# Attention with the keys on the partitions: row maxima by a product of high parts, no transposed probabilities, sums on GpSimd, one scaling per output

## The chip, the cores and the metric

The kernel runs on one core of a Trainium2 chip. A time is the device time of that core in microseconds (us), from the first to the last instruction of one launch with a small rest around it. A kernel's time is the median of several launches. Below, PE is TensorE (matmuls, with a separate engine row PEld for its weight loads), DVE is VectorE, ACT is ScalarE, POOL is GpSimd, and SP is the engine that issues most DMA transfers.

## What is computed

The reference is one layer of a hybrid network: 1024 latent tokens and 256 prompt tokens, width 1024, float32. A normalised and modulated input goes through one wide projection, then through two token mixers side by side (a gated linear recurrence called HGRN here, and attention), an output projection, and a squared-ReLU MLP. The change is in the attention:

```python
s = jnp.einsum('bqkgd,bskd->bkgqs', qi, kf) * scale   # 8 query heads on 2 key/value heads, 64 wide
p = jax.nn.softmax(s, axis=-1)
return jnp.einsum('bkgqs,bskd->bqkgd', p, vf)
```

Latent queries attend to 512 cached keys and the 1024 latent keys (1536 in all); prompt queries attend to the 256 prompt keys.

The kernel's matmuls take their operands in a format that the code calls F32R. A float32 operand x is split into a high part hi(x), which is x copied to that format, and a low part x - hi(x). A product of two split operands is three matmuls: high by high, high by low, low by high. With heads of 64 channels the kernel puts both parts of an operand on top of each other on 128 partitions, and gets the product with two matmuls.

## The kernel before

The program is built by one function. The order of PE's instructions is the order of the code; the instructions of the other engines and of the DMA queues are ordered by a scheduler that follows estimated times. Each engine runs its own list strictly in order, and waits at the first instruction whose operands or buffers are not ready.

The stages, in order: a front part (normalisation, the projection of keys, values and half of the queries), the projection of the other queries, the attention, the HGRN recurrence, output projections, the MLP, and the final normalisation. The matmuls of the attention and of HGRN are mixed with others: a "filler" is a generator that gives out the remaining parts of the wide projection (`z_ch`, `z_tok`, lines 316 to 347) a few matmuls at a time. `attention(fill)` (lines 787 to 811) makes a list of events, each with a due time in steps, sorts it, and before each event lets the filler advance to the same share of its total. So a stretch of PE's list holds attention matmuls and, evenly between them, filler matmuls (L312 to L314 and L329 to L331).

A `Unit` (lines 664 to 766) is one head and 256 queries, with the queries on the partitions. There are 32 units for latent queries and 8 for prompt queries. In a latent unit:

- `score`: for each block of 128 queries and each of three groups of 512 keys, two matmuls write 128 x 512 scores (L697), and DVE takes the maximum of each row (L698, L702).
- `expo`: ACT takes the exponential with the negative maximum as bias, and adds up the row (L708); DVE makes the reciprocal of the sum (L711, L712).
- `norm`: the exponentials are multiplied by that reciprocal, alternately on POOL and DVE (L716).
- `trans`: for two key blocks of 128 and two query blocks, four PE transposes (L738) bring the keys onto the partitions in PSUM; ACT copies the high part out (L741), DVE makes the low part (L742).
- `value`: high and low parts are multiplied with the values, 256 queries wide (L753, L754), and added up in one PSUM bank. At a unit's end ACT and DVE add the two halves of the result (L762, L763).

PSUM has eight banks, in three rings: "g" with three (filler, and the sum in `value`), "s" with three (scores), "t" with two (transposes). SBUF tiles come from rings too, with a buffer used again when its last reader is done. Ring X holds 20 tiles of 128 x 512 (keys and exponentials among them). Ring K holds a single tile: first `ident0`, then `R`, a constant pattern that the scans of HGRN read (L1091 to L1093, L874, L875). HGRN's preparation (`prep`, lines 865 to 931) runs on DVE and POOL and ends in the tile `usf`, which PE transposes in `keys_t` (L936) before any other matmul of that stage. The filler of HGRN (L1094) comes after that in PE's list.

## Time and profile before

| | |
|---|---|
| median of 3 runs (lowest to highest) | 2095.98 us (2095.45 to 2096.78) |
| the profiled execution's own time | 2093.83 us |
| its span, first to last instruction | 2092.1 us |
| mean granted PE clock | 0.995 |
| PE / DVE / ACT / POOL busy | 97% / 67% / 46% / 26% |
| first and last score matmul (L697) starts | 186.1 us, 730.2 us |
| last value matmul (L754) starts | 745.6 us |
| first HGRN scores (L947) start | 754.5 us |

The profile is one execution on the chip. The table of windows gives, for stretches of that execution, each engine's busy time. A group is all instructions of one line, engine and shape: count, then total busy us and mean ns of one, then the idle time of the engine just before them and who ended it. The chain is the work that ended last, followed back from the end, so its entries show what a matmul costs when the next one follows at once: PE is a pipeline, and the 390 ns of a matmul of 512 columns overlap with the next one's.

### The profile page before, as it was taken

To read this page: it belongs to the slowest core of one execution; us is meant where nothing else is said; L and a number is where in the kernel's file an instruction comes from. 1 tells how busy PE (TensorE), PEld (TensorE's weight loads), DVE (VectorE), ACT (ScalarE), POOL (GpSimd) and SP (SyncE) were. 2 spreads that over 40 slices of the span, in tenths; PEclk is the share of its full clock that TensorE was granted. 3 is DMA by queue.
4 is the path that set the end of the run, shared out by engine and by line. 5 is a ranking of instruction groups with operands and counts; after the bars stand their busy time and mean duration, and the time that the engine had idled before them with its cause. 6 is when DMAs were issued, how large, how long until landed. Compare 5 with 4: busy or idle time off the path is not lost.

```text
span 2092.1 us, 33337 instructions
## 1 busy us (share of the span) xinstructions
PE 2035.8 (97%) x12244; PEld 1748.0 (84%) x12244; DVE 1405.6 (67%) x2653; ACT 952.0 (46%) x1961; POOL 540.3 (26%) x577
## 2 busy tenths in 40 slices
PE   6899999999999999999999999999999999999998
PEld 4788889988889978888888888988888888888876
DVE  4784676776776797778354735776666666577686
ACT  4754555555565522322231425654454544333442
POOL 1472232333323355455212200222211210000010
PEclk9999999999999999999999999999999999999999
DMA  9455220232221355445644523774444479545773
GB/s 295 130 165 168 74 76 31 77 116 69 78 74 37 107 164 175 139 146 158 216 145 140 206 101 99 218 215 149 157 146 156 157 254 365 166 154 177 228 252 124
DMA packets 230243, 319.19 MB, mean 153 GB/s; under 512 B 18072, under 2 KB 148720, under 8 KB 230080
## 3 DMA queue, kind: packets, MB, share of 16 engines
q1 hardware_dynamic: 217664, 277.41, 41.4%
q0 software_dynamic: 12416, 39.66, 5.3%
q8 instruction: 96, 1.57, 0.3%
q14 instruction: 67, 0.55, 0.1%
HBM read 229.43 MB, written 87.57 MB: 152 GB/s over the span
## 4 chain that ended last, share of the span: by engine, by line
PE 83%; DVE 8%; DMA 5%; ACT 2%; issue 1%; SPq 0%; POOL 0%; DVEq 0%; POOLq 0%; ACTq 0%
PE ps_g L312 7%; PE ps_g L314 7%; PE ps_g L313 7%; PE ps_s L697 4%; PE ps_t L738 4%; PE ps_g L1591 2%; PE ps_g L1589 2%; PE ps_g L1590 2%; PE ps_g L754 2%; PE ps_s L1437 2%; PE ps_s L1438 2%; PE ps_s L1439 2%; DMA wraw<-in_w_ff 2%; PE ps_g L329 2%; PE ps_g L753 2%; PE ps_g L331 2%
## 5 line engine op out<-in xcount | busy, mean ns | idle before, releaser
L312 PE MATMUL ps_g<-hs,wsp 128*128 128x512 f32 (+1 forms) x896 | 322.3, 360 | 0.1
L314 PE MATMUL ps_g<-hs,wsp 128*128 128x512 f32 (+1 forms) x896 | 309.5, 345 | 0.8 <-DVE wsp L284 0.8
L313 PE MATMUL ps_g<-hs,wsp 128*128 128x512 f32 (+1 forms) x896 | 309.0, 345 | 0.0
L716 POOL TENSOR_SCALAR pexp<-pexp,rs 128x512 f32<-128x512 f32 (+1 forms) x104 | 170.2, 1643 | 375.6 <-ACT pTh L741 190.8
L283 ACT ACTIVATE wsp<-wraw 128x1024 fp32r<-128x1024 f32 x110 | 109.6, 998 | 262.8 <-PE ps_g L313 81.0
L284 DVE TENSOR_TENSOR wsp<-wraw,wsp 128x1024 fp32r<-128x1024 f32 x110 | 134.3, 1223 | 120.8 <-ACT wsp L283 120.4
L314 PEld LDWEIGHTS ps_g<-hs,wsp 128*128 128x128 f32 x896 | 169.3, 189 | 22.7 <-DVE wsp L284 1.0
L312 PEld LDWEIGHTS ps_g<-hs,wsp 128*128 128x128 f32 x896 | 169.7, 189 | 21.2 <-issue 4.6
L313 PEld LDWEIGHTS ps_g<-hs,wsp 128*128 128x128 f32 x896 | 170.0, 190 | 15.3
L741 ACT ACTIVATE pTh<-ps_t 128x512 fp32r<-128x512 f32 x200 | 118.9, 601 | 122.3 <-PE ps_t L738 119.3
L698 DVE TENSOR_REDUCE mx<-ps_s 128x1 f32<-128x512 f32 (+1 forms) x208 | 137.0, 663 | 53.9 <-PE ps_s L697 53.4
L283 ACT ACTIVATE ah<-ar 128x640 fp32r<-128x640 f32 (+1 forms) x112 | 80.9, 723 | 187.4 <-PE ps_g L1590 102.3
L708 ACT ACTIVATE pexp<-ps_s,ngm 128x512 f32<-128x512 f32 (+1 forms) x208 | 137.4, 669 | 43.2 <-DVE ngm L702 41.7
L742 DVE TENSOR_TENSOR pTl<-ps_t,pTh 128x512 fp32r<-128x512 f32 x200 | 136.0, 681 | 15.8 <-ACT pTh L741 15.4
L284 DVE TENSOR_TENSOR ah<-ar,ah 128x640 fp32r<-128x640 f32 (+1 forms) x112 | 90.1, 805 | 77.2 <-ACT ah L283 76.0
L697 PE MATMUL ps_s<-Kl,Ql 128*128 128x512 f32 (+1 forms) x416 | 128.9, 415 | 1.6 <-ACT pexp L708 1.6
L738 PE MATMUL ps_t<-ident,pexp 128*128 128x128 f32 x800 | 120.7, 273 | 2.5 <-DVE ngm L702 1.3
L329 PE MATMUL ps_g<-wsp,hs 128*128 128x256 f32 x400 | 117.5, 294 | 0.0
L331 PE MATMUL ps_g<-wsp,hs 128*128 128x256 f32 x400 | 113.7, 284 | 0.0
L330 PE MATMUL ps_g<-wsp,hs 128*128 128x256 f32 x400 | 113.6, 284 | 0.0
L754 PE MATMUL ps_g<-pTl,Vl 128*128 128x256 f32 x400 | 106.2, 286 | 3.6 <-DVE pTl L742 3.5
L753 PE MATMUL ps_g<-pTh,Vl 128*128 128x256 f32 x400 | 106.1, 285 | 1.3 <-DVE oa L763 1.1
(417 smaller groups left out, 5443.5 us busy)
## 6 DMA issues: line engine op xcount, KB each, us to landing
ar<-AF SPq DMA_DIRECT2D x112, 320.0 KB, 3.5
wraw<-in_w_ff SPq DMA_DIRECT2D x32, 1024.0 KB, 6.4
wr<-in_w_ff SPq DMA_DIRECT2D x128, 256.0 KB, 4.5
wraw<-in_w_in SPq DMA_DIRECT2D x18, 1024.0 KB, 5.5
wraw<-in_w_ada SPq DMA_DIRECT2D x16, 1024.0 KB, 5.5
AF<-a POOLq DMA_DIRECT2D x48, 256.0 KB, 2.8
AF<-t POOLq DMA_DIRECT2D x48, 256.0 KB, 2.3
wa<-in_w_ada SPq DMA_DIRECT2D x32, 256.0 KB, 5.8
```

Source lines behind the costliest of these rows:

```text
L283: s_.activation(hi, raw, AF.Copy)
L284: v.tensor_tensor(lo, raw, f32(hi), op=ALU.subtract)
L312: pe.matmul(out, hi[:, k, :], mh, start=(first and k == 0), stop=False)
L313: pe.matmul(out, hi[:, k, :], ml, start=False, stop=False)
L314: pe.matmul(out, lo[:, k, :], mh, start=False, stop=(last and k == kcs - 1))
L329: pe.matmul(po[:, bb, :], mh[:, off:off + P], wh[:, k % 4, :], start=(k == 0), stop=False)
L331: pe.matmul(po[:, bb, :], ml[:, off:off + P], wh[:, k % 4, :], start=False, stop=(k == KC - 1))
L697: pe.matmul(pq[:, 0:n], self.qh[:, q0:q0 + P], K[self.g][var][self.kts[i]], start=(var == 0), stop=(var == 1))
L716: NORM[(i + j) % len(NORM)].tensor_scalar(x, x, self.rs[j], None, op0=ALU.mult)
L738: pe.transpose(pt[:, a, j * P:(j + 1) * P], self.Ps[j][i][:, b * P:(b + 1) * P], ident)
L753: pe.matmul(pv[:, 0:256], V[self.g][kg][:, b, :], hi[:, a, :], start=(k == 0), stop=False)
L754: pe.matmul(pv[:, 0:256], V[self.g][kg][:, b, :], lo[:, a, :], start=False, stop=(k == last))
```

## The change

A unit now has the keys on the partitions, so no probability is transposed. There are 16 latent units of one head and 512 queries, with 12 key blocks of 128 each, and 4 prompt units of two heads and 256 queries each, with 2 key blocks: 200 blocks in all. In a unit:

- `top`: one matmul per 128 queries and key group, high parts of the keys by both parts of the queries (L707), and a DVE maximum of each row (L708). That is close to the true maximum, and only has to keep the exponential in range.
- `top_row`: a PE transpose turns the four columns of negative maxima into rows (L715), ACT copies them (L717), and four small DMAs write them into partition 64 of a second query operand `q2` (L719). `q2` holds the high part of the queries on partitions 0 to 63 and zeros below row 64; the low-part operand of the keys holds the low part, a row of ones and zeros. So the second score matmul adds low by high and the negative maximum.
- `score`: per key block two matmuls of 512 queries (L725), the exponential without bias or sum (L727), the high part by ACT from SBUF (L729), the low part by DVE from SBUF (L730). POOL adds the exponentials up over the blocks (L735, L737).
- `value`: high and low part by the values, 512 wide (L748), in a PSUM bank of its own ("v"); ring "g" has two banks during the attention.
- `sums`: four matmuls with one column (L759) add POOL's tile over the partitions; DVE takes the reciprocal. `scale`: a PE transpose (L766), an ACT copy into the tile `prow`, a DMA to memory and a DMA that spreads it to 64 partitions, both issued by POOL (L109, L772), and one POOL product with the unit's output (L773).

In the front part the high and low parts of the keys are made differently, three of the eight scalings of the prompt columns go from DVE to ACT, and the priority of one split is lowered. The norm weights `qkw`, `mrow` and `prow` share ring K with `ident0` and `R`.

```diff
-    PSB = {"g": 3, "s": 3, "t": 2}
+    PSB = {"g": 2, "v": 1, "s": 3, "t": 2}
...
-            if kc % 3 == 1:
+            if kc % 3 == 1 and t < 2:
...
-        v.tensor_tensor(st[:, :, 1], kb, f32(st[:, :, 0]), op=ALU.subtract)
+        v.tensor_tensor(st[:, :, 1, 0], kr, f32(st[:, :, 0, 0]), op=ALU.subtract)
+        s_.activation(st[:, :, 1, 1], one0.unsqueeze(1).broadcast_to([P, 2, 64]), AF.Copy)
...
-            with tc.high_priority(offset=600):
+            with tc.high_priority(offset=0):
...
+        def top(self, b, i):
...
+            pq = PS("t")
+            pe.matmul(pq[:, 0:n], self.q1[:, b * P:(b + 1) * P], K[self.g][0][self.kts[i]], start=True, stop=True)
+            v.tensor_reduce(self.mx[:, i:i + 1], pq[:, 0:n], axis=AX.X, op=ALU.max)
...
+        def top_row(self):
+            pt = PS("t")
+            pe.transpose(pt[0:4, 0:P], self.ngm, ident)
+            r = S((4, P), F32R, name="mrow")
+            s_.activation(r, pt[0:4, 0:P], AF.Copy)
+            for b in range(4):
+                dma(self.q2[64:65, b * P:(b + 1) * P], r[b:b + 1, :])
...
+        def score(self, k):
+            kg, b = self.kt[k]
+            pq = PS("s")
+            for var, q in enumerate((self.q1, self.q2)):
+                pe.matmul(pq, K[self.g][var][kg][:, b * P:(b + 1) * P], q, start=(var == 0), stop=(var == 1))
+            e = S(name="pexp")
+            s_.activation(e, pq, AF.Exp)
+            hi, lo = S(dt=F32R, name="pTh"), S(dt=F32R, name="pTl%d" % (k % 2))
+            s_.activation(hi, e, AF.Copy)
+            v.tensor_tensor(lo, e, f32(hi), op=ALU.subtract)
...
+                g_.tensor_tensor(self.acc, self.acc, e, op=ALU.add)
...
+        def scale(self):
+            pt = PS("t")
+            pe.transpose(pt[0:4, 0:P], self.rs, ident)
+            r = S((4, P), name="prow")
+            s_.activation(r, pt[0:4, 0:P], AF.Copy)
+            row = RR[self.h][self.t]
+            store(row.rearrange("o (b n) -> (o b) n", b=4), r)
+            o, rb = self.o, S((64, 512), name="prb")
+            g_.dma_start(out=rb, in_=row.broadcast_to([64, 512]))
+            g_.tensor_tensor(o, o, rb, op=ALU.mult)
...
+            ev += [(-12.9, u.load_q, ()), (-5.9, u.load_q2, ()), (-2.9, u.top_row, ())]
+            tops = [(b, i) for b in range(4) for i in range(len(u.kts))]
+            ev += [(-11.6 + 8.2 * j / len(tops), u.top, x) for j, x in enumerate(tops)]
+            ev += [(k, u.score, (k,)) for k in range(u.nb)]
+            ev += [(2 * p2 + 3.6, u.value, (p2,)) for p2 in range(u.nb // 2)]
+            ev += [(u.nb + 3.3, u.sums, ()), (u.nb + 4.3, u.scale, ())]
```

The numbers ahead of the events are due times in steps of one key block, counted from the unit's first score.

PE in the middle of the attention, before: value matmuls (L753, L754), four transposes of exponentials (L738), two scores of two matmuls each (L697), and filler (L312 to L314).

```order
L753 MATMUL ps_g<-pTh,Vl 128x256 [waits Activation_49]
L754 MATMUL ps_g<-pTl,Vl 128x256 [waits DVE_49]
L753 MATMUL ps_g<-pTh,Vl 128x256
L754 MATMUL ps_g<-pTl,Vl 128x256
L738 MATMUL ps_t<-ident,pexp 128x128 [waits PE_49]
L738 MATMUL ps_t<-ident,pexp 128x128 x3
L697 MATMUL ps_s<-Kl,Ql 128x512 [waits DMAHW7_49,DMAHW4_49,Activation_49]
L697 MATMUL ps_s<-Kl,Ql 128x512 [waits DMAHW0_49]
```

The same engine in the changed kernel: scores (L725) of one key block, values 512 wide (L748), the first block of the next unit with its second operand (Q_5293), and a matmul for a maximum (L707).

```order
L725 MATMUL ps_s<-Ql,Kl 128x512
L725 MATMUL ps_s<-Q_4953,Kl 128x512
L318 MATMUL ps_g<-hs,wsp 128x512
L319 MATMUL ps_g<-hs,wsp 128x512
L320 MATMUL ps_g<-hs,wsp 128x512
L748 MATMUL ps_v<-pTh,Vl 128x512 [waits Activation_49]
L748 MATMUL ps_v<-pTl_5336,Vl 128x512 [waits DVE_49]
L748 MATMUL ps_v<-pTh,Vl 128x512 [waits Activation_49]
L748 MATMUL ps_v<-pTl_5359,Vl 128x512 [waits DVE_49]
L725 MATMUL ps_s<-Ql,Kl 128x512
L725 MATMUL ps_s<-Q_5293,Kl 128x512 [waits DMAHW3_49,DMAHW4_49,DMAHW2_49,DMAHW7_49,DMAHW1_49,DMAHW0_49]
```

The transposes and the narrow value matmuls are gone, and a unit's first score waits for DMAs (the row of maxima among them).

POOL's list before, early in the program: the two memsets of `R` stand between the loads of the masks and the normalisation of the first rows (L254).

```order
L145 DMA mask_115<-const_masks 128x128
L891 MEMSET um 128x4x16 x2
L1092 MEMSET R 128x512
L254 TENSOR_TENSOR rst<-mm,mexp 128x4
L1093 MEMSET R 128x16
```

POOL's list of the changed kernel at the end of the attention: the last sums (L737), the last two DMAs of `scale` (RR_1_1951 is the row in memory, prb its copy on 64 partitions), the memsets of `R` (L1109, L1110), and the first products of HGRN (L900, L928) around the last scaling (L773).

```order
L737 TENSOR_TENSOR pacc<-pacc,pexp 128x512 [waits Activation_49,Pool_49] x3
L868 TENSOR_TENSOR ze<-ze,hnb 128x512 [waits DMAHW6_49,DVE_49]
L109 DMA RR_1_1951<-prow 4x128 [waits Activation_49]
L868 TENSOR_TENSOR ze<-ze,hnb 128x512 [waits DMAHW7_49,DVE_49]
L772 DMA prb<-RR_1_1951 64x512 [waits DMASW0_49,PE_49]
L1109 MEMSET R 128x512 [waits DMAHW4_49,DMAHW3_49,DMAHW5_49,DMAHW2_49,DMAHW6_49,DMAHW1_49,DMAHW0_49]
L1110 MEMSET R 128x16 [waits Pool_49]
L900 TENSOR_SCALAR uf<-uf 128x512 [waits DMAHW6_49,DVE_49,PE_49]
L773 TENSOR_TENSOR oa<-oa,prb 64x512 [waits DMAHW2_49,DMASW1_49]
L928 TENSOR_TENSOR usf<-uf,usf 128x512 [waits DVE_49,Pool_49]
```

`R` has moved from the start of POOL's list to behind the last `prow` of the attention, because both are in ring K.

SP's list of the changed kernel around the row of maxima of one unit (Q_4953 is its `q2`, QS the stored queries, OA the stored outputs of earlier units, KS the stored keys).

```order
L106 DMA Q_4953<-QS_1_139 64x512 [waits DMAHW5_49,PE_49,Activation_49]
L106 DMA OA_2_1928<-oa 64x2x256 [waits DMAHW6_49,Pool_49]
L106 DMA Q_4953<-mrow 1x16x8 [waits DMAHW7_49,Activation_49]
L106 DMA Q_4953<-mrow 1x16x8 [waits DMAHW0_49]
L106 DMA Q_4953<-mrow 1x16x8 [waits DMAHW1_49]
L106 DMA Q_4953<-mrow 1x16x8 [waits DMAHW2_49]
L106 DMA Kl<-KS_141 128x512 [waits DMAHW3_49,DMASW1_49,DVE_49]
```

The four small DMAs are new, and ahead of them stands a store that waits for POOL's product of an earlier unit.

More of the change, by code (lines that the diff above doesn't have):

```diff
@@ L618, in build @@
                 front_prep(evs)
[L619 removed]
+            banks = [PS(x) for x in ("sssv", "ggss", "sv")[t]]
         cols_next = t == 0 and kc % 2 == 1 and kc < KC - 1
@@ L765, in value @@
-            if self.h % 2 == 1 and self.q2 == n // 256 - 1:
-                dma(OA[self.h // 2][self.t], o_at[self.h // 2, self.t][:, 0:n])
-    NORM = [g_, v]
-    q_at, o_at = {}, {}
+                self.pv = PS("v")
+            last = self.nb - 1
+            for k in (2 * p2, 2 * p2 + 1):
+                kg, b = self.kt[k]
+                for j, x in enumerate(self.pt.pop(k)):
+                    pe.matmul(self.pv, V[self.g][kg][:, b, :], x, start=(k == 0 and j == 0), stop=(k == last and j == 1))
@@ new lines, in value, with sums @@
+            if k == last:
+                tm, self.o = S((64, 512), name="pvt"), S((64, 512), name="oa")
+                with tc.high_priority(offset=400):
+                    s_.activation(tm, self.pv[64:128], AF.Copy)
+                    v.tensor_tensor(self.o, self.pv[0:64], tm, op=ALU.add)
+        def sums(self):
+            pt = PS("t")
+            for b in range(4):
+                pe.matmul(pt[:, b:b + 1], self.acc[:, b * P:(b + 1) * P], one0[:, 0:1], start=True, stop=True)
+            self.rs = T(4, "rs")
+            v.reciprocal(self.rs, pt[:, 0:4])
```

180 lines of the change are left out of this document (66 added, 114 removed), and 5 rows, old and new, of the table RING_OF.

## The prediction

> **What bounds the kernel now.** I read the page first, then the table of windows around the attention, then the chain inside it.
>
> ```profile
> PE 2035.8 (97%) x12244; PEld 1748.0 (84%) x12244; DVE 1405.6 (67%) x2653; ACT 952.0 (46%) x1961; POOL 540.3 (26%) x577
> 196.00:740.00 544.00, 536.82 (x3788) 485.30 (x3788) 383.83 (x834) 308.48 (x734) 180.52 (x113) 1.00 0.22 73
> 740.00:755.00 15.00, 11.09 (x81) 8.95 (x85) 14.84 (x27) 4.68 (x10) 9.88 (x9) 0.89 0.54 180
> 755.00:1025.00 270.00, 267.63 (x2169) 226.16 (x2162) 211.61 (x492) 74.35 (x191) 136.85 (x160) 1.00 0.51 161
> ```
>
> The window rows hold length, then busy time of PE, PEld, DVE, ACT and POOL, the clock, DMA. In the attention (196 to 740 us) PE is busy 536.8 of 544 us, DVE 71%, POOL 33%; in HGRN (755 to 1025) PE is busy 267.6 of 270. So a matmul less in the attention shortens the program, and a wait of PE at its end lengthens it one to one. Busy time hides short gaps, so I cost matmuls by the chain, where an entry is the time until the next matmul starts:
>
> ```profile
> 602.32 0.44 PE ps_t L738 x4
> 602.76 0.94 PE ps_s L697 x4
> 603.70 0.23 PE ps_g L312
> ...
> 731.98 0.11 PE ps_g L753
> 732.09 0.12 PE ps_g L754
> ```
>
> 512 columns cost 0.23 us, 256 columns 0.12, and a bundle of four transposes 0.44.
>
> **The change on PE.** The groups give the counts:
>
> ```profile
> L697 PE MATMUL ps_s<-Kl,Ql 128*128 128x512 f32 x384 | 121.9, 424 | 1.6 <-ACT pexp L708 1.6
> L697 PE MATMUL ps_s<-Kl,Ql 128*128 128x256 f32 x32 | 7.1, 302 | 0.0
> L738 PE MATMUL ps_t<-ident,pexp 128*128 128x128 f32 x800 | 120.7, 273 | 2.5 <-DVE ngm L702 1.3 <-DVE pexp L716 1.3
> L754 PE MATMUL ps_g<-pTl,Vl 128*128 128x256 f32 x400 | 106.2, 286 | 3.6 <-DVE pTl L742 3.5
> ```
>
> Before: scores 384 x 0.233 + 32 x 0.12 = 93.3 us; transposes 200 x 0.44 = 88; values 800 x 0.12 = 96 (L753 has as many as L754). Sum 277.3. After, with 200 blocks: scores 400 x 0.233 = 93.2; values 400 x 0.233 = 93.2, nothing saved although they are half as many; maxima 192 x 0.233 + 16 x 0.12 = 46.7. Each of the 20 units adds two single transposes and four one-column matmuls. None of these exists before; the nearest row is the bundle of 0.44, of which 0.35 is transposes and 0.09 the slower start behind it, so 0.44 for the four and 0.18 for each single: 0.8 x 20 = 16 us, bounds 8 and 25. Sum 249. **PE saves 28 us** (19 to 36).
>
> **What the other engines do.** These rows price the parts that lie beside PE:
>
> ```profile
> L742 DVE TENSOR_TENSOR pTl<-ps_t,pTh 128x512 fp32r<-128x512 f32 x200 | 136.0, 681 | 15.8 <-ACT pTh L741 15.4
> L698 DVE TENSOR_REDUCE mx<-ps_s 128x1 f32<-128x512 f32 x192 | 130.3, 683 | 51.1 <-PE ps_s L697 50.7
> L708 ACT ACTIVATE pexp<-ps_s,ngm 128x512 f32<-128x512 f32 x192 | 129.8, 686 | 41.2 <-DVE ngm L702 40.8
> L283 ACT ACTIVATE wh<-wr 128x512 fp32r<-128x512 f32 x32 | 19.7, 617 | 0.0
> L851 POOL TENSOR_TENSOR ze<-ze,hnb 128x512 f32<-128x512 f32 x10 | 13.0, 1304 | 15.8 <-DVE ze L849 8.3 <-PE ps_t L738 5.1 <-DVE ngm L702 2.2
> L104 POOL DMA_DIRECT2D AF<-a x48 | 26.0, 541 | 145.0 <-ACT a L1339 145.0
> ```
>
> The stage's first and last attention matmuls, from the views of their lines (min, median and max ns, then first and last start):
>
> ```profile
> L697 PE MATMUL ps_s<-Kl,Ql x416: 277/399/505, 186.1 to 730.2; 128*128 128x512 f32 x128, 128*128 128x256 f32 x11
> L754 PE MATMUL ps_g<-pTl,Vl x400: 277/282/580, 205.9 to 745.6; 128*128 128x256 f32 x134
> ```
>
> The attention (559.5 us from L697's first start to L754's last, less 28) has 217.7 steps, so a step is 2.44 us, some 2.5 where blocks run. ACT needs 0.69 + 0.62 per block, about as before: hidden. POOL needs 1.30 per sum, 11 sums per unit of 12 steps, and some 6 us for the scaling (two issues of 0.54, a landing of 2.5 as below, a product, a short wait): 20 of 30 us, hidden. `sums` stands 4.3 steps (11 us) behind the last score, more than the 2.6 us of exponential and last sum. The row of maxima has 2.9 steps (7 us) for a transpose, a copy, four DMA issues and a landing (the DMA rows end with the us from issue to landing):
>
> ```profile
> out_new_state_hgrn<-ust SPq DMA_DIRECT2D x8, 64.0 KB, 1.6
> GR<-gt POOLq DMA_DIRECT2D x1, 16.0 KB, 2.5
> OA<-oa SPq DMA_DIRECT2D x8, 256.0 KB, 2.0
> ...
> 729.45 0.44 SPq L101 DMA_DIRECT2D uq<-QD  x1
> ```
>
> With issues of 0.44 us (the last row, from the timeline) and a landing of 1.6 to 2.5 that is 4 to 5 us. The store of OA ahead of it on SP waits for POOL's product, due 4.8 steps earlier; all SP traffic queues behind it if POOL is late. I take no loss here; if the cover fails, each us late costs 20 us over the units. Ring X (20 tiles) and the "t" ring (2 banks for the maxima) are tighter than before; against that, the chain maximum, exponential, sum, reciprocal, norm, transpose is gone. PE's idle time in the window is 7 us. I allow 7 us more within the stage (bounds -5 and 25).
>
> **What the change adds at the end.** `R` now stands behind the last `prow` on POOL, and HGRN's scans need it:
>
> ```profile
> 733.77 1.13 DVE ucp L874
> 734.90 1.11 DVE usf L875
> 749.84 1.31 DVE usf L907
> 751.20 0.66 PE ps_t L936 x4
> L1092 POOL MEMSET R<- x1: 571/571/571, 7.2 to 7.2; 128x512 f32 x1
> ```
>
> Before, the first scan started at 733.8 us, beside the last value matmuls, and 17.4 us later PE had its first transpose of HGRN. After, the scan can start only when the last rs is transposed (0.3), copied (0.3, as the small copy below), issued (0.54, L104), landed (2.5, the row of GR), the next DMA issued and `R` set (0.6 + 0.6): 5 us. From scan to transpose I take 11 us of the 17.4, since some 3 us of low parts and outputs (L742, L763) lay between. That is 16 us, of which PE has 2 to 3 us of filler left. Against this PE lost 4 us in the 15 us window of before. So the end costs **8 us more** (bounds 4 and 14). That window's clock of 0.89 shows that PE also runs slower around such gaps. The Trainium skill, "TensorE: Matmul & The Clock Gate", section on the HAM clock gate, has PE fall to half its clock after an idle window of about 3.4 us and stay there as long: by it a gap of 13 us would cost an estimated 1.7 us more, within my bounds.
>
> **The front part** (0 to 118 us) is edited too.
>
> ```profile
> 0.00:118.00 118.00, 89.87 (x529) 68.69 (x529) 74.69 (x176) 69.32 (x158) 40.84 (x62) 0.96 0.66 205
> L191 ACT ACTIVATE modc<-ps_g,cols 128x2 f32<-128x2 f32 x18 | 3.8, 266 | 5.4 <-PE ps_g L188 5.4
> L1059 ACT ACTIVATE ze<-ps_g 128x512 f32<-128x512 f32 x32 | 19.1, 598 | 78.5 <-PE ps_g L314 67.6 <-issue 7.7 <-DMA GD<-ze 1.4
> ```
>
> PE is busy 90 of 118 us there, so ACT or DVE can delay it. 14 small copies (0.27 to 0.60 us each by these rows) and three scalings go to ACT, less goes to DVE, and each engine has over 40 us free: 0, bounds -3 and 3. Two banks instead of three for the filler cost nothing, since `value` held the third for most of the stage before; if that cover fails, a 0.60 us evacuation (L1059) shows some 40 times. After the attention the third bank is back.
>
> **The sum.** -28 + 7 + 8 = -13 us. The profiled execution took 2093.8 (1.7 more than its span), so 2080.8; the median is 2.2 above it, so 2083, and I say 2082.
>
> **The rivals.** *All is hidden:* without the 7, and with HGRN's preparation overlapped better than I think, -28 gives 2068. For it: DVE loses the norms and row sums. Against it: the order of POOL's list.
>
> *Slower: DVE and POOL hold each other up.* Low parts were taken from PSUM, now from two SBUF tiles, while POOL adds two SBUF tiles. Two operations of before show this meeting:
>
> ```profile
> 742.79 1.01 DVE L898 TENSOR_TENSOR um<-um,ucp 128x4 f32<-128x4 f32 x1
> 744.90 0.15 DVE L901 TENSOR_TENSOR udec<-um,ucp 128x4 f32<-128x4 f32 x1
> 742.28 1.49 POOL L907 TENSOR_TENSOR uf<-usf,um 128x512 f32<-128x512 f32 x1
> 643.36 0.68 DVE L698 TENSOR_REDUCE mx<-ps_s 128x1 f32<-128x512 f32 x1
> 643.96 0.68 DVE L742 TENSOR_TENSOR pTl<-ps_t,pTh 128x512 fp32r<-128x512 f32 x1
> ```
>
> A 128x4 product took 1.01 us beside POOL's product and ended 0.03 us after it; its like took 0.15 with POOL idle. The Trainium skill, "SBUF — State Buffer", section "Who interferes with whom", says that a DVE instruction with two SBUF inputs and a GpSimd instruction that reads SBUF exclude each other, and the later one waits for the whole of the first; the trace agrees. In the change POOL's sum and ACT's high part start together behind the exponential, so a low part finds POOL about 0.6 us into its 1.30 and waits 0.7. DVE's instructions start 0.60 apart (the last two rows). In the dense 8.2 of 12 steps DVE then has 1.46 maxima x 0.60, a low part of 0.60 and other work of 0.2: 1.7 us, and 2.4 with the wait, just under the 2.5 of a step. That is why I don't forecast it. It decides above a wait of 0.8 us. At 1.05 (POOL late, and slowed by DVE in turn) each of 131 dense steps is 0.25 longer: 33 us more, so 2115.
>
> *No change:* the stalls within the stage reach 17 to 25 us instead of 7: 2092 to 2100. That the change does less than it says is no rival: the lists hold 40 transposes where there were 800.
>
> **How the numbers follow.** A measurement of this kernel tells 0.2% (4 us) from no change. Forecast, 2073 to 2090: 0.45. All hidden, 2060 to 2073: 0.17. No change, 2090 to 2100: 0.17. DVE and POOL, 2100 to 2130: 0.21. Faster than 2091.8: 0.45 + 0.17 + 0.02 = 0.64; within 4 us 0.14; slower 0.22. The range leaves out the ends of both outer cases: 2063 to 2108.
>
> **What would show it.** Right: L738 gone; first score to last value about 530 us; before HGRN's first transpose (L953) PE idle 10 to 14 us behind the last L766, with L1109 just ahead of the first scan; L730 means 1.2 to 1.4 us, POOL's L737 1.3 to 1.6. Wrong: PE waiting at L707 for DVE or at L725 for ACT in every unit (the slower rival), at L725's second operand for DMA (SP's queue), or no gap at L953 (all hidden).

## The result, and the profile after

| | before | after |
|---|---|---|
| median of the runs | 2096.38 us (2095.45 to 2097.63, 4 runs) | 2115.36 us (2113.45 to 2128.83, 4 runs) |
| profiled execution | 2093.83 us, span 2092.1 | 2115.53 us, span 2113.4 |
| mean granted clock | 0.995 | 0.990 |

The change makes the kernel slower: ratio 1.0104, 95% interval 1.0062 to 1.0146. A second set of runs (e5 below) gave 1.0117 (1.0102 to 1.0132). The forecast was 2082 us, with a range of 2063 to 2108.

The page's first part and the windows that answer to those shown of before; the columns are length, PE, PEld, DVE, ACT, POOL, clock, DMA:

```profile
PE 2015.6 (95%) x11436; PEld 1696.6 (80%) x11436; DVE 1437.2 (68%) x2385; ACT 958.2 (45%) x1802; POOL 675.8 (32%) x715
```

```profile
196.00:740.00 544.00, 514.89 (x2949) 432.56 (x2948) 411.69 (x560) 313.22 (x564) 311.27 (x244) 0.99 0.27 82
740.00:755.00 15.00, 7.02 (x66) 6.17 (x64) 2.78 (x4) 2.90 (x5) 6.18 (x8) 0.85 0.53 166
755.00:771.00 16.00, 0.00 (x0) 0.00 (x0) 14.21 (x22) 1.06 (x1) 8.47 (x8) 0.50 0.47 156
771.00:1041.00 270.00, 266.71 (x2127) 224.16 (x2128) 210.35 (x488) 69.95 (x180) 140.98 (x161) 0.99 0.49 153
```

PE is busy for 20 us less in the whole run (2015.6 against 2035.8), and yet the run is longer. The second and third rows show one place: from 747 to 771 us PE does nothing, and from 755 on DVE works instead (14.2 of 16 us in the third row). The fourth row is HGRN, which runs as before. The first row shows the other place, less plainly: PE is idle for 29 us of the attention, where it was idle for 7.

The first and the last matmul of the attention's blocks, from the views of their lines (the last two numbers are first and last start):

```profile
L725 PE MATMUL ps_s<-Ql,Kl x192: 387/394/497, 196.6 to 734.6; 128*128 128x512 f32 x192
```

```profile
L748 PE MATMUL ps_v<-pTl,Vl x200: 387/393/628, 205.3 to 740.0; 128*128 128x512 f32 x100
```

So the last value matmul starts at 740.0 us, where it started at 745.6 before: 5.6 us earlier. HGRN's first transpose follows 31.2 us later (771.2), where it followed 5.6 us later before: 25.6 us lost. From there to the end it is 1342.2 us against 1340.9. That is the account: -5.6 + 25.6 + 1.3 = 21.3 us, the difference of the spans.

The 5.6 us are not the attention's gain. Ahead of it stand the transposes of the queries, and PE has as many matmuls up to the last of them in both kernels (969 in the views). Their rows, before and after, and then the windows up to that transpose and from there to the last value (before: the first two rows, and a third for the stretch from the last value to HGRN's first transpose; after: the last two):

```profile
L485 PE MATMUL ps_t<-ident,qst x80: 220/243/281, 93.6 to 179.8; 128*128 128x128 f32 x80
L492 PE MATMUL ps_t<-ident,qst x80: 222/243/253, 92.3 to 175.1; 128*128 128x128 f32 x80
```

```profile
0.00:179.80 179.80, 151.67 (x969) 125.93 (x969) 113.20 (x250) 101.48 (x230) 71.06 (x94) 0.96 0.66 201
179.80:745.60 565.80, 556.65 (x3904) 501.46 (x3902) 396.10 (x857) 316.74 (x752) 187.23 (x118) 1.00 0.24 77
745.60:751.20 5.60, 3.47 (x33) 2.60 (x31) 5.54 (x10) 1.85 (x6) 2.74 (x2) 0.90 0.23 76
0.00:175.10 175.10, 147.46 (x969) 121.86 (x970) 109.26 (x246) 105.62 (x248) 68.81 (x94) 0.99 0.67 206
175.10:740.00 564.90, 534.16 (x3057) 447.87 (x3056) 422.02 (x578) 317.42 (x573) 311.27 (x244) 0.99 0.28 85
```

So 4.7 of the 5.6 us lie ahead of the attention. They are no saved work: the granted clock of that stretch is 0.96 before and 0.99 after, an estimated 5 us of 180. In e5, the changed kernel again, the same transpose starts at 178.0 us, and in e2 to e4 at 176.8 to 178.9. From that transpose to the last value PE is busy for 22.5 us less and idle for 21.6 us more. Of the 22.5 us, 3.5 only moved behind the last value, where PE is busy for 7.02 us up to HGRN (the row 740.00:755.00 above) and was for 3.47. What the matmuls saved is therefore some 19 us.

What PE waited for between 196 and 735 us, first before, then after (us in total, times, longest):

```profile
PE ps_g L754 <- DVE pTl L742: 2.3, 4, 1.0
...
```

```profile
PE ps_t L707 <- DMA Qp<-QS: 6.1, 4, 2.8
PE ps_t L707 <- DMA Ql<-QS: 5.7, 4, 3.5
PE ps_t L707 <- DVE mx L708: 4.5, 7, 1.6
PE ps_t L715 <- DVE ngm L710: 4.2, 6, 1.2
...
PE ps_s L725 <- DMA Ql<-QS: 2.8, 1, 2.8
...
```

In all it is 6.5 us before (four rows) and 29.0 after (eight): 22.5 us more. Half of the 29.0 are for loads of queries (14.6 us, the first, the second and the last row shown), a third for the maxima on DVE (8.7, the third and the fourth). No row is large and most come a few times, so no single wait stands in every unit.

The end, in the chain of waits after (start, length, what), one row of POOL's timeline, and, from SP's timeline before, the loads of the same `uf` and of the first of the same weights:

```profile
745.50 1.24 DVE wsp L290
746.75 0.38 SPq L106
747.23 0.53 SPq L106
747.87 8.73 DMA uf<-FD
...
766.68 1.99 DVE ucp L891
...
770.11 0.99 DVE usf L924
771.23 1.09 PE ps_t L953 x4
```

```profile
749.30 0.54 POOL L1109 MEMSET R<- 128x512 f32 x1
```

```profile
728.98 0.42 SPq L101 DMA_DIRECT2D uf<-FD  x1
...
748.52 0.38 SPq L101 DMA_DIRECT2D wraw<-in_w_ada  x1
```

`R` was set by 750.0 us, 5.3 after the last L766 (744.7): the forecast's 5 us. But the chain does not go through it. It goes through SP: two weight loads of 1 MB (746.75 and 747.23) wait for the split of the weights before them (L290), and the first unit's `uf` is the next load on that queue. It landed at 756.6, and only then did the first scan run (before, this load was issued 20 us ahead of those weights). Between the scan and the transposes stand DVE's other work for that unit and the second unit's scans (L891 at 766.68), ahead of the first unit's last product (L924).

The two groups that the slower rival spoke of:

```profile
L730 DVE TENSOR_TENSOR pTl<-pexp,pTh 128x512 fp32r<-128x512 f32 x199 | 228.3, 1150 | 48.5 <-ACT pTh L729 47.1
```

```profile
L737 POOL TENSOR_TENSOR pacc<-pacc,pexp 128x512 f32<-128x512 f32 x160 | 230.2, 1439 | 111.7 <-ACT pexp L727 68.6 <-ACT prow L768 30.0 <-ACT mrow L717 9.0
```

A low part takes 1150 ns against 681 before, a sum 1439 against the 1304 of POOL's product before.

### The profile page after: what moved, and what is told of

It is laid out like the page before. It is cut to its first block, busy times and chain, and to the rows that moved or that the text cites. A ratio compares the mean times of both kernels' runs of the same rounds, so it can differ in the third digit from the quotient of the medians.

```text
span 2113.4 us, 31691 instructions
## 1 busy us (share of the span) xinstructions
PE 2015.6 (95%) x11436; PEld 1696.6 (80%) x11436; DVE 1437.2 (68%) x2385; ACT 958.2 (45%) x1802; POOL 675.8 (32%) x715
## 4 chain that ended last, share of the span: by engine, by line
PE 42%; issue 15%; POOL 4%; DVE 3%; DMA 2%; ACT 1%; SPq 0%; POOLq 0%; DVEq 0%; ACTq 0%
POOL AF L109 4%; PE ps_g L318 3%; PE ps_g L319 3%; PE ps_g L320 3%; PE ps_s L1606 2%; PE ps_s L1607 2%; PE ps_s L1608 2%; PE ps_v L318 1%; PE ps_g L1608 1%; PE ps_t L1606 1%; PE ps_g L1606 1%; PE ps_g L1607 1%; PE ps_t L1607 1%; PE ps_t L1608 1%; PE ps_v L320 1%
## 5 line engine op out<-in xcount | busy, mean ns | idle before, releaser
L737 POOL TENSOR_TENSOR pacc<-pacc,pexp 128x512 f32<-128x512 f32 x160 | 230.2, 1439 | 111.7 <-ACT pexp L727 68.6
L730 DVE TENSOR_TENSOR pTl<-pexp,pTh 128x512 fp32r<-128x512 f32 x200 | 229.8, 1152 | 48.7 <-ACT pTh L729 47.3
L318 PE MATMUL ps_g<-hs,wsp 128*128 128x512 f32 (+1 forms) x688 | 249.9, 363 | 0.0
L320 PE MATMUL ps_g<-hs,wsp 128*128 128x512 f32 (+1 forms) x688 | 241.6, 351 | 0.8 <-DVE wsp L290 0.8
L319 PE MATMUL ps_g<-hs,wsp 128*128 128x512 f32 (+1 forms) x688 | 241.8, 351 | 0.0
L290 DVE TENSOR_TENSOR wsp<-wraw,wsp 128x1024 fp32r<-128x1024 f32 x110 | 139.2, 1266 | 130.4 <-ACT wsp L289 130.1
L727 ACT ACTIVATE pexp<-ps_s 128x512 f32<-128x512 f32 x200 | 119.3, 597 | 163.9 <-PE ps_s L725 124.7
L708 DVE TENSOR_REDUCE mx<-ps_t 128x1 f32<-128x512 f32 (+1 forms) x208 | 136.8, 664 | 72.5 <-PE ps_t L707 71.7
L318 PEld LDWEIGHTS ps_g<-hs,wsp 128*128 128x128 f32 x688 | 131.4, 191 | 20.3 <-issue 2.9
L320 PEld LDWEIGHTS ps_g<-hs,wsp 128*128 128x128 f32 x688 | 131.0, 190 | 18.9 <-DVE wsp L290 1.0
L290 DVE TENSOR_TENSOR ah<-ar,ah 128x640 fp32r<-128x640 f32 (+1 forms) x112 | 89.8, 802 | 80.4 <-ACT ah L289 79.2
L319 PEld LDWEIGHTS ps_g<-hs,wsp 128*128 128x128 f32 x688 | 131.3, 191 | 16.5
L729 ACT ACTIVATE pTh<-pexp 128x512 fp32r<-128x512 f32 x200 | 126.0, 630 | 7.6
L707 PE MATMUL ps_t<-Kl,Ql 128*128 128x512 f32 x192 | 78.6, 410 | 12.5 <-DMA Ql<-QS 5.7
L725 PE MATMUL ps_s<-Q,Kl 128*128 128x512 f32 x200 | 79.0, 395 | 5.8 <-DMA Q<-mrow 3.0
L336 PEld LDWEIGHTS ps_g<-wsp,hs 128*128 128x128 f32 x400 | 75.9, 190 | 6.6
```

The costliest lines, as they stand in the source:

```text
L290: v.tensor_tensor(lo, raw, f32(hi), op=ALU.subtract)
L318: pe.matmul(out, hi[:, k, :], mh, start=(first and k == 0), stop=False)
L319: pe.matmul(out, hi[:, k, :], ml, start=False, stop=False)
L320: pe.matmul(out, lo[:, k, :], mh, start=False, stop=(last and k == kcs - 1))
L336: pe.matmul(po[:, bb, :], mh[:, off:off + P], wl[:, k % 4, :], start=False, stop=False)
L708: v.tensor_reduce(self.mx[:, i:i + 1], pq[:, 0:n], axis=AX.X, op=ALU.max)
```

## The experiments

All edits are made on the changed kernel, alone or together. Ratios are to the kernel before, run on the same chip in turn; 0.001 is 2.1 us.

| run | what | median us | ratio (95%) |
|---|---|---|---|
| e5 | the change again | 2118.92 | 1.0117 (1.0102 to 1.0132) |
| e1 | R early | 2125.27 | 1.0143 (1.0124 to 1.0162) |
| e2 | uf early | 2120.88 | 1.0125 (1.0109 to 1.0140) |
| e3 | both | 2127.95 | 1.0152 (1.0127 to 1.0177) |
| e4 | OA stored by POOL | 2134.50 | 1.0187 (1.0170 to 1.0204) |
| e6 | R early, first preparation early | 2111.49 | 1.0081 (1.0062 to 1.0100) |
| e7 | maxima later | 2117.65 | 1.0109 (1.0089 to 1.0130) |
| e8 | no sums | 2107.83 | 1.0057 (1.0040 to 1.0075) |
| e9 | low part from PSUM | 2103.80 | 1.0039 (1.0027 to 1.0052) |
| e10 | e9 and e7 | 2098.37 | 1.0027 (1.0012 to 1.0042) |
| e11 | e6, second unit too | 2111.43 | 1.0084 (1.0070 to 1.0098) |
| e12 | e10 and e11 | 2086.19 | 0.9959 (0.9947 to 0.9972) |
| e13 | e11, second unit behind the scaling | 2108.32 | 1.0057 (1.0045 to 1.0070) |
| e14 | e10 and e13 | 2080.16 | 0.9933 (0.9922 to 0.9945) |
| e15 | e9 with a smaller ring X | 2122.86 | 1.0138 (1.0125 to 1.0151) |

### The end: R, the load, or the lists (e1, e2, e3)

Theory A is the prediction's: the first scan waits for `R`, behind the last `prow`. Theory B came out of the chain above: it waits for `uf`, behind two weight loads. In e1 `R` has a ring of its own (one tile) and is set ahead of the attention:

```
-    "usm": "B", "ust": "D", "uo1": "E", "ukt": "F", "uo": "G", "ojk": "J", "oT": "I", "R": "K",
+    "usm": "B", "ust": "D", "uo1": "E", "ukt": "F", "uo": "G", "ojk": "J", "oT": "I", "R": "L",
...
+    R = S(name="R")
+    g_.memset(R, 0.0)
+    g_.memset(R.rearrange("p (c i) -> p c i", i=32)[:, :, 0:1], 1.0)
```

> R gets a ring of its own and is set before the attention, so the scans no longer stand behind the last row of reciprocals (prow); nothing else is edited. Theory A, the prediction's (the chain prow, RR, R holds HGRN's first scan): R was set at 750.0 us, so the first scan moves from 756.7 to about 740 and the kernel gains 8 to 15 us: 2100 to 2107. Theory B (the first scan waits for its input uf, whose load stands on SP behind two 1 MB weight loads and landed at 756.6): R was ready 6.6 us before uf, so the scan stays at 755 to 757, PE's gap ahead of L953 stays 24 us, and the time is 2113 to 2116.

Ratio 1.0143, and the end stands as it was. The waits of PE and of DVE at the end of e1:

```profile
PE ps_t L956 <- DVE usf L927: 24.4, 1, 24.4
```

```profile
DVE ucp L894 <- DMA uf<-FD: 9.5, 1, 9.5
```

`R` is there from the start, the scan still waits 9.5 us for `uf`, and PE's gap is 24.4 us instead of 24.2. So theory A fails: `R` is not what comes last. Against the change itself e1 is 0.3% up, with intervals that overlap; its attention is longer (537.6 us from the first to the last value matmul, 532.3 in e5), and why was not settled.

In e2 the loads of HGRN's first two units are issued within the attention, and `R` stays where the change has it:

```
+    def preload(t):
+        f, q = PRE[0, 0, t] = S(name="uf"), S(name="uq")
+        dma(f, FD[0][0][t])
+        dma(q, QD[0][t])
...
+        events += [(s0 - 7.0, preload, (0,)), (s0 - 5.0, preload, (1,))]
```

(`prep` then takes these tiles.)

> The loads uf and uq of HGRN's first two units are issued 5 and 7 steps before the end of the attention, ahead of the two weight loads on SP; R stays behind prow. Theory A (R holds the scan): no gain, 2113 to 2116. Theory B: uf lands by about 740, then R at 750.0 is what comes last, so the first scan moves from 756.7 to about 750, PE's gap shrinks from 24 to about 17.5 us, and the time is 2108 to 2110.

PE's wait at the first transposes fell to 19.6 us (17.5 expected), and DVE's first scan now waits 2.6 us for `R`. But the time did not follow: 1.0125, with 540.8 us from the first to the last value.

e3 has both edits.

> Both edits: R set early and uf loaded ahead of the weights. If the end of the attention is the loss that the sum missed, the first scan comes before 740, PE's gap ahead of L953 falls from 24 us to under 6, and the time is 2094 to 2099: 17 to 21 us less than the change. If the two edits only add up as single prices under theory A (8 to 15 and 0), it is 2100 to 2107.

Ratio 1.0152, and PE still waits 22.9 us: theory B, too, is wrong in this simple form. DVE's timeline of e3 shows why (start, length; L866, L891, L895 and L924 of the change have the numbers L877, L904, L908 and L937 here; L891 and L895 are the scan in its two directions):

```profile
758.26 1.23 DVE L290 TENSOR_TENSOR wsp<-wraw,wsp 128x1024 fp32r<-128x1024 f32 x1 [1.97 <-ACT wsp L289]
...
760.11 1.22 DVE L904 TENSOR_TENSOR_SCAN ucp<-R,uf 128x512 f32<-128x512 f32 x1
...
776.74 2.28 DVE L908 TENSOR_TENSOR_SCAN ucp<-R,uf 128x512 f32<-128x512 f32 x1
...
781.07 1.47 DVE L937 TENSOR_TENSOR usf<-usf,um 128x512 f32<-128x512 f32 x1
```

`R` and `uf` had long been there (the loads were issued at 736.5), but in DVE's list the first scan stands behind the filler's last weight split and evacuation, which need PE's last filler matmuls. And a scan of the third unit (L908) stands ahead of the product that PE waits for. This gave theory C: three locks stand in a row, R, the load, and the places in the lists of DVE and POOL, and opening one or two shows the next. The attention of e3 is longer too, 543.0 us from the first to the last value. The early loads of e2 and e3 take tiles of ring X, which the attention uses; whether that is the reason was not tested.

### The stores of OA (e4)

```
-                dma(oa[d0:d0 + 64, :], o)
+                store(oa[d0:d0 + 64, :], o)
```

(Likewise for t of 2; `store` issues on POOL's queue.)

> OA is stored from POOL's queue, right behind POOL's product, so that no store on SP waits for POOL (128 us of SP's waits within the attention, 19 of them); one issue of 0.55 us more per unit on POOL. Theory: the loads of Ql, Qp and the rows mrow stand on SP behind those stores, and PE's 17.6 us of waits for them in the attention fall to under 6: 2100 to 2105. Rival: the loads wait for their buffers or for the other stores on SP (VD, GD, 88 us behind DVE alone), or other waits take their place: 2111 to 2116.

1.0187, the slowest of all. The waits for queries stayed (Ql 6.8, Qp 6.2, mrow 5.1 us), so the stores of OA were not what held the loads up: the forecast's "no loss" for them was right. Of the 15 us by which its ratio stands above that of e5, 9.5 are a single new wait of PE at L748. That wait, and the chain of e4:

```profile
PE ps_v L748 <- ACT pTh L729: 9.5, 1, 9.5
```

```profile
699.94 9.99 DMA wraw<-in_w_in
709.95 1.06 ACT wsp L289
...
```

ACT reaches the split of a weight that is still landing, and PE waits 9.5 us for the high part that stands behind that split in ACT's list; the low part behind DVE's half of the split then costs 0.9 more. It is the same kind of lock as at the end.

### The change again, and the first preparation moved (e5, e6)

> The changed kernel as it is, on the chip of this call, so that the three others are compared with it on one chip. The four runs so far were between 2113.5 and 2128.8 us; if the kernels of the first call lost 6 to 20 us by their edits, this one is at 2113 to 2117 again; if part of that was the chip, it is at 2117 to 2122.

2118.92, some 3 us more than in the first runs; e1 and e3 remain a little above it in their ratios. PE's waits in e5 up to 775 us, with which those of e6 to e9 are compared (further down in that view, `ngm` at L715 makes 4.5 us and the row of maxima at L725 3.0):

```profile
PE ps_t L707 <- DMA Qp<-QS: 6.9, 4, 3.2
PE ps_t L707 <- DMA Ql<-QS: 5.8, 4, 3.8
PE ps_t L707 <- DVE mx L708: 4.9, 7, 1.6
...
```

In e6 the whole preparation of HGRN's first unit is issued within the attention:

```
+    def preprep():
+        HU.append(HUnit(0, 0, 0))
+        HU[0].prep()
...
+        events += [(s0 - 6.0, preload, ()), (s0 - 0.5, preprep, ())]
...
-        units[0].prep()
```

(`hgrn` then takes `HU[0]`; R as in e1.)

> R set early as in e1, the loads uf and uq of HGRN's first unit issued 6 steps before the end of the attention's scores, and that unit's whole preparation (scans, factors, products on DVE and POOL) issued half a step before their end, so that the lists of DVE and POOL have it ahead of the last sum, the last rs, prow and the filler's last weights. Theory C (PE's gap at the end comes from where HGRN's first preparation stands in the lists of DVE, POOL and SP, R being one of three locks in a row): the gap of 24 us ahead of HGRN's first transpose falls under 6, and the kernel takes 16 to 22 us less than the change on the same chip. Rival: the next unit's preparation is late instead, PE's idle time moves behind the first transposes, and under 8 us are gained.

1.0081, 7.5 us less than e5. The gap of 24.2 is gone, but the longest of PE's waits around the end is the rival's:

```profile
PE ps_t L972 <- DVE usf L943: 8.1, 1, 8.1
```

The second unit's transposes now wait 8.1 us: its `uf` had become the load behind the weights (9.2 us from issue to landing). Theory C holds for the first unit; the second needs the same.

### The waits within the stage (e7, e8, e9, e10)

e7 issues a unit's maxima one step later, so that the loads of the queries have longer:

```
-            ev += [(-11.6 + 8.2 * j / len(tops), u.top, x) for j, x in enumerate(tops)]
+            ev += [(-10.6 + 7.2 * j / len(tops), u.top, x) for j, x in enumerate(tops)]
```

> A unit's maxima are issued from 10.6 steps ahead of its first score instead of 11.6, ending as before (3.6 to 3.4 steps ahead), so the load of Ql or Qp has 2.3 steps (5.9 us) instead of 1.3 (3.3 us) before its first use. Theory: PE's 14.6 us of waits for Ql and Qp come from that lead; they fall under 5 us, and 7 to 10 us are gained against the change on the same chip. Rival: the loads start late on SP (their buffers come free late, other stores stand ahead), or the denser maxima make PE wait for DVE instead: within 4 us of the change.

1.0109, the same as e5 within the intervals: the rival. The waits of PE in e7 (to 775 us):

```profile
PE ps_t L707 <- DVE mx L708: 9.9, 16, 1.7
...
PE ps_t L707 <- DMA Ql<-QS: 2.0, 1, 2.0
...
```

The lead was what the loads lacked: the waits for them ahead of the maxima fell from 12.7 us in e5 to 2.7. But those for `mx` rose from 4.9 to 9.9, and those for mrow from 3.0 to 5.1. DVE was right behind.

e8 leaves out POOL's sums, so its outputs lack the real scaling; it only serves as a measurement:

```
-            if k == 0:
-                self.acc = e
...
+            if k == 1:
+                self.acc = S(name="pacc")
+                g_.memset(self.acc, 1.0)
```

> POOL's sums (L735, L737) are left out; the accumulator is set to one instead, by one memset per unit, so the outputs are not scaled by the real sums. Theory D (DVE and POOL hold each other up): the low parts fall from a mean of 1152 ns to about 690, PE's 8.7 us of waits for mx and ngm vanish, prow and the scaling come earlier, and 8 to 20 us are gained against the change on the same chip. Rival: DVE's longer low parts lie beside PE's work (DVE 76% busy), so L730 gets shorter and the time changes by less than 4 us.

1.0057, 12.6 us less than e5 by the ratios. DVE's group in e8:

```profile
L730 DVE TENSOR_TENSOR pTl<-pexp,pTh 128x512 fp32r<-128x512 f32 x200 | 142.6, 713 | 84.6 <-ACT pTh L729 83.5
```

The low parts are at 713 ns, and of PE's waits for `mx` and `ngm` 0.9 us are left of 9.4. Theory D holds: DVE's longer low parts are paid for. Whether it is the meeting of operands or POOL's time that costs, e8 alone does not say; e9 keeps the sums and takes one operand of the low part from PSUM:

```
-            e = S(name="pexp")
-            s_.activation(e, pq, AF.Exp)
+            s_.activation(pq, pq, AF.Exp)
...
-            s_.activation(hi, e, AF.Copy)
-            v.tensor_tensor(lo, e, f32(hi), op=ALU.subtract)
+            s_.activation(hi, pq, AF.Copy)
+            v.tensor_tensor(lo, pq, f32(hi), op=ALU.subtract)
+            e = f32(hi)
```

(POOL's sums take `e`, which is now the high part, so the row sums leave out the low parts.)

> The exponential is written in place into the score bank; the high part is copied from there, the low part is PSUM minus SBUF as before the change, and POOL sums the high parts (the row sums leave out the low parts). Theory D (two SBUF operands on DVE beside POOL's sum): L730's mean falls from 1152 ns to about 700 with POOL's sums still running, PE's 9.4 us of waits for mx and ngm fall under 3, and the ratio to before falls from 1.0117 to 1.005 to 1.008, as without the sums (1.0057). Rival (the sums cost by POOL's time, not by the operands): the low parts stay above 1 us and the ratio stays at 1.010 to 1.014. A score bank is held some 1.3 us longer, which could cost ACT or PE a wait at the three score banks: then a ratio of 1.008 to 1.012 with the low parts at 0.7.

1.0039, 16 us less than e5, with POOL's sums running. DVE's and POOL's groups in e9:

```profile
L729 DVE TENSOR_TENSOR pTl<-ps_s,pTh 128x512 fp32r<-128x512 f32 x198 | 135.5, 686 | 77.9 <-ACT pTh L728 76.6
```

```profile
L737 POOL TENSOR_TENSOR pacc<-pacc,pTh 128x512 f32<-128x512 f32 x160 | 209.9, 1312 | 105.7 <-ACT pTh L728 88.8 <-ACT prow L768 7.7 <-ACT mrow L717 4.0
```

One operand moved from SBUF to PSUM takes 464 ns off each low part and 127 off each sum. The Trainium skill, "SBUF — State Buffer", section "Who interferes with whom", says that a DVE instruction with two SBUF inputs and a GpSimd instruction that reads SBUF exclude each other for the whole of the one that came first; by that rule a PSUM operand ends it on both sides, and these rows agree.

> Low parts from PSUM as in e9 and the later maxima of e7 together. Theory: the loads of Ql and Qp and the waits for mx are two limits of one stretch, so that either edit alone mostly uncovers the other; together PE's waits for Ql, Qp (12.7 us), mx and ngm (9.4) all fall to under 6, and the ratio is 5 to 9 us (0.0025 to 0.0045) under that of e9. Rival: the edits add up as they did alone, e7's gain of 1.3 us on top of e9's.

1.0027 against e9's 1.0039, with overlapping intervals: 2.5 us by the ratios, not 5 to 9. The waits for Ql, Qp, `mx` and `ngm` come to 12.1 us where e9 has 14.1. That the two hide each other is not what limits this stage any more; what does is open.

### Ring X as another reason for e9 (e15)

```
-RINGS = {"X": 20, "I": 4, "B": 4, "D": 3, "E": 3, "F": 2, "G": 2, "J": 1, "K": 1}
+RINGS = {"X": 16, "I": 4, "B": 4, "D": 3, "E": 3, "F": 2, "G": 2, "J": 1, "K": 1}
```

> As e9 (low parts from PSUM, sums of the high parts) with 16 tiles in ring X instead of 20. e9 takes one X tile per block where the change takes two, so its gain could be the ring's and not the operands'. Theory D (operands): L729's mean stays at 0.69 us and the ratio at 1.003 to 1.006. Rival (ring X): with 4 tiles less PE waits for ACT's exponentials and the loads that use X (Qp, the second operands), and the ratio goes back to 1.009 to 1.013.

The ratio, 1.0138, is the rival's, but the place is not the rival's place. In the attention PE's waits are as in e9 and the low parts are as fast; the loss that can be pointed to is behind it, in HGRN, which uses ring X as well. DVE's group within the attention and PE's waits from 770 us on:

```profile
L729 DVE TENSOR_TENSOR pTl<-ps_s,pTh 128x512 fp32r<-128x512 f32 x194 | 133.0, 687 | 75.2 <-ACT pTh L728 73.8
```

```profile
PE ps_t L953 <- DVE usf L924: 13.1, 3, 8.5
```

e9 has 2.0 us of that wait. So e9's gain within the attention is the operands', not the ring's. Of the 22 us by which the two spans differ, 13.3 lie behind HGRN's first transpose (1354.0 us to the end, 1340.7 in e9), 2.7 between the first and the last value (522.4 against 519.7), and 6.3 ahead of the attention's first value (212.2 against 205.9), where the granted clock is 0.97 in e15 and 0.99 in e9.

### The end, opened to the last lock (e11 to e14)

In e11 the second unit is prepared early as well:

```
+        events += [(s0 - 6.0, preload, (0,)), (s0 - 5.0, preload, (1,))]
+        events += [(s0 - 0.5, preprep, (0,)), (s0 + 3.0, preprep, (1,))]
```

> As e6, and for HGRN's second unit too: its loads 5 steps ahead of the end of the scores, its preparation 3 steps behind it. Theory C: in e6 PE stood 8.1 us ahead of the second unit's transposes, since its uf was the load behind the two weight loads (landing 9.2 us); that gap goes too, PE's idle time from the last value to the last transposes falls from e6's 13.6 to under 7, and the ratio is 1.003 to 1.006 (e6 1.0081, the change 1.0117). Rival: the gap moves on to the third unit, and the ratio stays at 1.007 to 1.009.

1.0084, nothing better than e6. The gap ahead of HGRN is gone, but another stands in the attention's own last step:

```profile
PE ps_t L766 <- DVE rs L761: 8.9, 1, 8.9
```

DVE's list now has the second unit's scans ahead of the last `rs`. e12 puts this together with e10.

> Low parts from PSUM, later maxima, R early and the first two units prepared early, together. If the stage's waits (22 us more idle time than before the change) and the end (22 us more) are the whole of what the sum missed, and the edits remove 12 to 18 and 14 to 18 of them, the kernel is at or under the one before: ratio 0.992 to 0.999. If part of each only moves elsewhere, 1.000 to 1.004.

0.9959: faster than the kernel before, with the same wait at L766 (9.7 us) still in it. So the second preparation goes behind the scaling:

```
-        events += [(s0 - 0.5, preprep, (0,)), (s0 + 3.0, preprep, (1,))]
+        events += [(s0 - 0.5, preprep, (0,)), (s0 + 4.4, preprep, (1,))]
```

> As e11, but the second unit's preparation is issued behind the scaling of the last unit (4.4 steps after the last scores instead of 3.0), so that the last rs (L761) no longer stands behind its scans on DVE; there is nothing else of e9 or e7 in it. Theory C: in e11 PE stood 8.9 us at L766 for rs, the last part of the end's gap; now its idle time from the last value to the first transposes falls from 11.0 us to under 4, the attention's own stays at 30 to 35, and the ratio is 1.003 to 1.006 (e11 1.0084, the change 1.0117). Rival: the second unit's preparation becomes late as in e6, and the ratio stays at 1.007 to 1.009.

1.0057: 12.6 us less than e5 from the end alone, within what was expected. PE waits 2.8 us at L766 and 0.2 at HGRN's first transposes. Not all of the 24 us came back: from the first to the last value the attention takes 545.8 us, 532.3 in e5. PE is idle there for 8.6 us more and busy for 4.9 more, at a granted clock of 0.98 instead of 0.99. Part of it are the last low parts, which stand behind the early scans (4.5 us of PE's waits at L748, 1.5 in e5); the rest was not traced.

> As e12 with the second unit's preparation behind the scaling, as in e13. Theory: e12's 9.7 us of PE at L766 for rs go, 5 to 9 us less than e12: a ratio of 0.991 to 0.994 to before. Rival: the second unit is late instead, 0.995 to 0.997.

0.9933 (0.9922 to 0.9945): 14 us faster than the kernel before. The longest of PE's waits between 170 and 800 us in e14, and the one at the end:

```profile
PE ps_t L707 <- DVE mx L708: 4.4, 7, 1.3
...
PE ps_t L766 <- DVE rs L761: 2.8, 1, 2.8
...
```

From e10 to e14 the end's edits are worth 19.7 us, against 12.6 from e5 to e13; that DVE's shorter low parts leave more room for the scans is a likely reason, and not tested by itself. From e5 to e10 the stage's edits are worth 18.8. Together they are 38.5 us, and with most of both losses taken out the change gains 14 us, half of the 28 that were forecast for its matmuls.

## Why the prediction was wrong, point by point

In the forecast's terms the 21.3 us are: matmuls -19 (-28 forecast), stalls in the stage +21.6 (+7), the end +22.1 (+8; the 25.6 us less the 3.5 of moved work), the front part -4.7 (0), and +1.3 behind. So the stalls and the end each came out some 14 us above their terms, the matmuls 9.

**The matmuls: mis-sized, at the low bound.** 28 us were forecast (19 to 36), and some 19 came. Of the 9 us that are missing, an estimated 3.4 are two stretches at half the clock (the end of this section), in which PE is busy for longer. And the four one-column matmuls of a unit run as eight, 160 in 20 units, and take 0.78 us together in the chain at the end, where 0.44 was priced for four:

```profile
742.52 0.78 PE ps_t L759 x8
```

The single transposes beside them cost less than the 0.18 priced (L766 at 744.69 is followed at 744.71). Which other terms are short was not traced.

**Stalls within the stage: mis-sized.** 7 us were allowed; 22.5 came by the waits, 21.6 by the windows, inside the bounds of -5 and 25. Two terms were missing. The load of `Ql` or `Qp` was not priced at all: it has 1.3 steps before its first maximum, and PE waited 14.6 us for these loads. And the meeting of DVE and POOL was taken as free below a wait of 0.8 us per low part, since a mean step had room for it. The wait was 0.47 us (1150 against 681), and it cost 12.6 us (e8) to 16 (e9). That dense stretches run over a step while the mean still fits is the likely reason; no run shows the single steps. The two terms do not simply add up, as e7 and e10 showed.

**The end: the step that failed.** "After, the scan can start only when the last rs is transposed ... and `R` set: 5 us" was right for `R` and wrong as the chain: e1 took `R` out and the gap stayed at 24.4 us. I had priced the one lock that the diff moved and took the rest of the preparation as staying where it was in the lists. It did not: before, `uf` was issued at 729 us on SP ahead of the weights and the first scan stood in DVE's list beside the last values. After, the load is behind the weights and the scans are behind the filler's last split. The price is 25.6 us (22.1 without the moved work) and not 8 (4 to 14); and 8 is a little low by its own figures, 16 less 2 to 3 and less 4, which make 9 to 10. "From scan to transpose I take 11 us" was short too: 14.5 (756.7 to 771.2), with the second unit's scans in between.

**What would show it.** The last value 530 us behind the first score: 543.4. PE idle for 10 to 14 us ahead of L953: 24.2. L1109 just ahead of the first scan: it was 7 us ahead. L730 at 1.2 to 1.4 us: 1.15; L737 at 1.3 to 1.6: 1.44. PE waiting for DVE at L707 in every unit: 7 times in all.

**The rivals.** The slower rival had the mechanism and came to the same time (2115), but its sum was another: 33 us from a point of decision, where e8 and e9 show 12.6 to 16 with a wait of 0.47 us, short of that point. That its 2115 was met is luck. As large a part of the error as the stalls' stood at the end, for which no slower rival was written. "No change" came closest on the stage: stalls of 17 to 25; its time was missed because of the end.

**The clock behind a gap.** After the 24 us without work PE's matmuls of 512 columns take 0.43 us each and then 0.23, in the chain:

```profile
772.32 0.43 PE ps_g L318
...
774.98 0.24 PE ps_g L319
```

So PE runs at half speed from 771.2 to about 774.5 us. The Trainium skill, "TensorE: Matmul & The Clock Gate", section on the HAM clock gate, has half the clock for one window of about 3.4 us after an idle one; the trace agrees at this gap, and the estimated 1.7 us are right in size. In e3, behind a gap of 22.9 us, the same matmuls take 0.43 us until 788.5, which is 5.8 us.

The clock also falls inside the stage, which the forecast left out. One of PE's waits for queries in the changed kernel, and the window behind it (the clock is the third number from the end):

```profile
573.02 0.71 PE L725 MATMUL ps_s<-Q,Kl 128*128 128x512 f32 x1 [2.84 <-DMA Ql<-QS]
```

```profile
573.10:576.50 3.40, 3.40 (x8) 2.67 (x9) 3.33 (x3) 2.79 (x6) 1.28 (x1) 0.50 0.00 0
```

Behind this wait of 2.8 us PE works for 3.4 us at half the clock, an estimated 1.7 us on top of the wait. The same follows the wait of 2.8 us that ends at 500.2 us (a clock of 0.50 from 501.4 to 504.8). The longest wait of the stage, 3.5 us up to 434.9, is not followed by such a stretch, so a stall's full cost can't be read from its length alone.

## What to carry to other kernels

When a change removes work that sets the pace of several in-order lists, the next stage's loads and preparations move in those lists too: read in the lists where the first instruction of the next stage stands on every engine and queue, and not only behind what the diff moved. A subtraction with one operand in PSUM instead of two in SBUF cost nothing here and was not slowed by GpSimd's adds (686 ns, 681 before). An edit that opens one or two of several locks in a row shows no gain (e1, e2, e3), so such edits are judged together and by where the wait went.

## What the runs showed of the hardware that was not expected

- A scan on DVE (two SBUF operands, 128x512) took 1.22 us with POOL idle and 2.06 to 2.28 beside POOL's products (the change at 766.60, e3 at 776.74).
- A load of 256 KB issued right behind two of 1 MB on the same queue took 8.7 to 9.2 us to land (the change, e1, e6); the median of the change's 16 loads of that size from the same tensor is 4.3.
